# A modulation unit is computed one unit after its load, queued on VectorE behind the last weight unit's low half

## The chip, the core and the metric

The kernel runs on one core of a Trainium2 chip. The metric is the device time of one execution in microseconds (us); a time is the median of several executions. The engines of the core work side by side, each on its own instruction queue in order: PE (TensorE, matrix products), DVE (VectorE), ACT (ScalarE), POOL (GpSimd) and SP (SyncE, which here issues the loads). An instruction waits in its queue until what it needs is there, and everything behind it on the same engine waits with it.

## The reference

Two transformer blocks on 256 tokens of width 2048, all in float32. Each block begins with a modulation: a vector `c` is multiplied with a wide matrix, and the products scale, shift and gate the activations. These products are matrix-vector products; all others have 256 rows.

```python
c_act = silu(c)
mod = c_act @ w_ada + b_ada                      # 2048 x 12288: sh_a, sc_a, gt_a, sh_f, sc_f, gt_f
h = rms_norm(x, g_attn) * (1 + sc_a) + sh_a
x = x + gt_a * parallel_mixers(h, w_in, ..., w_o)  # sparse and dense attention, gated, merged
h = rms_norm(x, g_ffn) * (1 + sc_f) + sh_f
x = x + gt_f * conv_ffn(h, w_up, w_conv, w_down)   # width 5632, 3-tap convolution over tokens
...
shift, scale, gate = split(silu(c_2) @ w_mod + b_mod, 3)   # 2048 x 6144
h = rms_norm(x) * (1 + scale) + shift
x = x + gate * pool_mixer(h, pool_w_in, pool_w_grp, pool_scale, pool_w_out)
out = rms_norm(x) * final_norm_g
```

## The kernel before

**Weight units.** Every weight matrix streams through the core once, in tiles of 128 x 1024 float32 (512 KB: two blocks of 128 rows by 512 columns). One such tile is a weight unit. `load_split` takes a `raw` buffer, loads the tile on SP (L275), lets ScalarE cast it to a high half (L158) and VectorE subtract the high half from the tile, which gives the low half (`tt` in `split`, recorded as L80). Both halves lie in an `hl` buffer. TensorE then does 12 matmuls (L380): two halves of the tokens by two row blocks by three products, high by high, high by low, low by high. There are 564 weight units. The ring of `raw` buffers has 6 (`NRAW`), that of `hl` buffers 5 (`NHL`); a load waits on SP until its `raw` buffer is free, which for a weight unit is when its low half is computed.

**Modulation units.** The matrix-vector products run on VectorE. A modulation unit is one 512 KB tile of `w_ada` or `w_mod`: a `raw` buffer from the same ring, a load on SP (L174), and one fused multiply with row sum on VectorE (L176, `vec_unit`), whose end frees the buffer. There are 288. `job_vec` puts them into the deque `jobs`; after the last unit of a vector it adds the two halves of the sums and calls `fin`, which makes a scale (`A1`, `A2`, `A3`), a shift or a gate row from them. Inside `gemm_gen`, behind each weight unit, `credit` grows by `rate` (0.4 to 1.05, by stage) and `pump(1)` takes one modulation unit for each full credit. `pump_to` and `pump(1000)` take many at once where a vector must be complete.

**What sets the order.** Outside an opening that is written by hand, the scheduler of the Tile framework places each instruction on its engine by its own model of when it can run, not by the line at which the program asks for it. `tc.issue_after(x)` keeps an instruction behind `x` in the queue of the engine, without a wait of its own. Before, a modulation product has one such edge, behind `gate[0]`, a copy in the norm at the start of a stage.

**Stages.** In the order of time: opening and input projection `w_in` (to about 640 us with the attentions; modulation units of `w_ada` at rates 1.05 and 0.5 to 1), `w_o` and the norm of the FFN (to about 740 us), `w_up` and `w_down` interleaved, with the convolution on `cv` tiles (to about 1430 us, modulation units at 0.45 and 0.4), the pool mixer with its input projection into `pu` (split into `puh` and `pul`), the group product `z` and its transpose `zT` (to about 1625 us, rate 0.5), and `pool_w_out`. `hN` are the normalised activations of a stage, high and low halves; `u` is the result of `w_up` ahead of the convolution; `gTlo` the low half of the gated product.

Of the kernel before, what the change touches and what calls it, by code (L numbers as in the profile page):

```python
# [14 lines left out]
OP = mybir.AluOpType  # L15
# [14 lines left out]
def block_pair_kernel(ctx: ExitStack, tc: tile.TileContext, T: dict, out: bass.AP):  # L30
    nc = tc.nc
    V, SC, PE, GP = nc.vector, nc.scalar, nc.tensor, nc.gpsimd
# [9 lines left out]
    NH, RH = 4, 0.9  # L42
    NF = 1
    NS4, NRAW, NHL = 28, 6, 5
    n_s4 = [0]
    WU = (1, 30, 2, 3)

# [31 lines left out]
    def tt(o, a, b, op):  # L79
        return V.tensor_tensor(o, a, b, op=op)  # L80
# [42 lines left out]
    cact = {}  # L123
# [32 lines left out]

    def split(hi, lo, src):
        SC.copy(hi, src)  # L158
        tt(lo, src, hi, OP.subtract)


    jobs = deque()
    gate = [None]

    def pump(n):
        for _ in range(n):
            if not jobs:
                return
            jobs.popleft()()

    def vec_unit(W, ct, h, cv, acc):

        raw = raw_tile()
        nc.sync.dma_start(raw, T[W][ct, h])  # L174
        with tc.issue_after(gate[0]) if gate[0] is not None else nullcontext():
            V.scalar_tensor_tensor(raw, raw, 1.0, cact[cv][h], op0=OP.mult, op1=OP.mult, accum_out=acc)  # L176

    def job_vec(W, cv, cts, fin):

        n = len(cts)  # L180
        st = {}

        def unit(i, h):
            if i == 0 and h == 0:
                n_s4[0] += 1
                st["vs"] = sp.tile([128, 2, 128], F32, name=f"vs_{n_s4[0]}", tag="vs", bufs=2)[:, :, :n]
            vs = st["vs"]
            vec_unit(W, cts[i], h, cv, vs[:, h, i:i + 1])
            if i == n - 1 and h == 1:
                tt(vs[:, 0], vs[:, 0], vs[:, 1], OP.add)  # L190
                fin(vs[:, 0])
        for i in range(n):
            for h in range(2):
                jobs.append(lambda i=i, h=h: unit(i, h))
# [77 lines left out]
    def load_split(blk, n, big=False):  # L272

        raw = raw_tile()
        nc.sync.dma_start(raw[:, :KT * n], blk)  # L275
        rv = raw[:, :KT * n].rearrange("p (k n) -> p k n", k=KT)
        if big:
            hl = [s4([128, KT, 512], F32R, name="hl")[:, :, :n] for _ in range(2)]
        else:
            n_s4[0] += 1  # L280
            t = sp.tile([128, 2, KT, 512], F32R, name=f"hl_{n_s4[0]}", tag="hl", bufs=NHL)
            hl = [t[:, b, :, :n] for b in range(2)]
        split(hl[0], hl[1], rv)
        return hl


# [81 lines left out]
    def gemm_gen(st, W, k0, nk, evac, rate=0.0, tail=0, head=0, kw=None, n=512, pre=(), ps=None,  # L368
                 part=(True, True)):


        ps = ps or [ps_mm(), ps_mm()]
        nu = nk // KT
        u0 = (k0 if kw is None else kw) // KT

        def mms(t, hl, u):
            for i in range(KT):
                k = u * KT + i
                for x, (a, b) in enumerate(((0, 0), (0, 1), (1, 0))):
                    PE.matmul(ps[t][:, :n], lhsT=st(k0 + k, t, a), rhs=hl[b][:, i, :],  # L380
                              start=(part[0] and k == 0 and x == 0), stop=(part[1] and k == nk - 1 and x == 2))
        late = []
        for u in range(nu):
            hl = pre[u] if u < len(pre) else load_split(W[u0 + u], n, big=u >= nu - tail)
            mms(0, hl, u)
            if u >= nu - tail or u < head:
                late.append((hl, u))
            else:
                mms(1, hl, u)
            if u == head - 1:  # L390
                for a in late:
                    mms(1, *a)
                late.clear()
            credit[0] += rate
            while credit[0] >= 1.0:
                pump(1)
                credit[0] -= 1.0
            if u < nu - 1:
                yield
        evac(0, ps[0])  # L400
        for a in late:
            mms(1, *a)
        evac(1, ps[1])
        yield
# [4 lines left out]
    acc = {}  # L409
# [28 lines left out]
    for g in range(NG):  # L438
# [9 lines left out]
        if g == 0:  # L448
# [16 lines left out]
            rest = 2 * math.pi  # L465
# [99 lines left out]
    for q in range(2):  # L565
        a = acc[QI0 + q]
# [14 lines left out]
    for t in range(2):  # L581
# [4 lines left out]
        for b in range(16 // hb):  # L586
            p = ps_at([128, hb, ns], name="dots")
            for i in range(hb):
                h = b * hb + i
# [5 lines left out]
            for i in range(hb):  # L595
                h = b * hb + i
# [8 lines left out]
        for r in range(8):  # L605
            src = score if r == 0 else work
# [35 lines left out]
    for j in range(3):  # L642
        src, c0 = (acc[LAT], j * 256) if j < 2 else (misc, 80)
# [4 lines left out]
        h = t2([128, 2, 256], name="lat32")  # L648
# [10 lines left out]
    for j in range(4):  # L659
        a = s4([128, 2, 384], name="mq")  # L660
        lat_gens.append(gemm_gen(stl, T["w_mq_up"][j], 0, 4, lambda t, p, a=a: SC.copy(a[:, t, :], p[:, :384]),
                                 n=384, rate=R4))
        mq.append(a)
    for j in range(4):
        a = s4([128, 2, 512], name="mkv")
# [28 lines left out]
    for q in range(2):  # L694
        a = acc[Q0 + q]
        rope_a(a, 4, tqa)
        o = s4([128, 4, 256], name="qaT")
        for j in range(2):
            p = ps_tp([128, 2, 256])
            for i in range(2):  # L700
                for t in range(2):
                    h = j * 2 + i
# [22 lines left out]
    for t in range(2):  # L725
        ns = 128 * (t + 1)
        for g in range(2):
            P = s4([128, 4, 256], name="pA")
            hb = 512 // ns
            for b in range(4 // hb):  # L730
                ps = ps_at([128, hb, ns], name="lgA")
                for i in range(hb):
                    h = b * hb + i
# [48 lines left out]
    for t in range(2):  # L782
        j = t2([128, 512], name="junk")
        SC.activation(j[:, :64], misc[:, t, 336:400], AF.Square, accum_out=ssr[:, t:t + 1])
        for jj in range(4):
            for h in range(2):
                j = t2([128, 512], name="junk")
                SC.activation(j[:, :192], mq[jj][:, t, h * 192:(h + 1) * 192], AF.Square,
                              accum_out=ssb[:, 0, t, jj * 2 + h:jj * 2 + h + 1])
# [3 lines left out]
                                       accum_out=ssb[:, 1, t, jj * 2 + h:jj * 2 + h + 1])  # L793
# [334 lines left out]
    for i in range(4):  # L1128
# [14 lines left out]
        for b in range(2):  # L1143
            p = ps_tp([128, 2, 256])
            for q in range(2):
                f = b * 2 + q
                n = 0
# [6 lines left out]
        hi = s4([128, 4, 256], F32R, name="plhi")  # L1154
        lo = s4([128, 4, 256], F32R, name="pllo")
# [162 lines left out]
```

## Time and profile before

| | |
|---|---|
| median of 3 runs | 1737.88 us (1735.26 to 1742.14) |
| profiled execution | 1738.78 us, span 1736.9 us |
| granted TensorE clock, mean | 0.993 |
| busy: PE / DVE / ACT / POOL | 97% / 79% / 52% / 1% |
| moved by DMA | 459.80 MB, mean 265 GB/s |

The span is what the profiler recorded; the execution is 1.9 us longer. Busy shares are means over all stages. "Idle before" in a row is the time in which the engine did nothing just ahead of that instruction, and the name behind the arrow is what ended last before it could start.

### The profile page before, as it was taken

What the parts mean: (1) busy time and instruction counts of PE and PEld (TensorE: products, weight loads), DVE (VectorE), ACT (ScalarE), POOL (GpSimd) and SP (SyncE); (2) the same over time, 40 slices, a digit from 0 to 9 for tenths busy, and PEclk for the clock granted to TensorE, in tenths of its full rate; (3) what the DMA queues carried; (4) which work ended last, traced back from release to release, by engine and by line L of the source; (5) the groups of instructions that cost most, each with busy time, mean ns of one, the idle gap of its engine ahead of it and who ended that gap; (6) DMA issues with size and microseconds to landing.
All of it is one profiled execution on the core that took longest, in us unless ns stands there. A gap on an engine that the chain in (4) does not pass through costs nothing.

```text
span 1736.9 us, 21934 instructions
## 1 busy us (share of the span) xinstructions
PE 1679.3 (97%) x7736; PEld 1375.3 (79%) x7736; DVE 1368.9 (79%) x2079; ACT 906.2 (52%) x1275; POOL 12.7 (1%) x29
## 2 busy tenths in 40 slices
PE   8899999999999989999989999999999999999997
PEld 6688888778778868788878878887888777888886
DVE  8899899998978778599677776777877877765765
ACT  4644354767854456555445544555345575454443
POOL 0000000000000000000000000000000000000000
PEclk9999999999999999999999999999999999999999
DMA  8999998678878858677877787777877748788762
GB/s 326 353 335 328 330 325 282 215 270 302 288 233 316 290 205 320 219 237 245 298 255 256 253 273 261 259 245 257 273 259 253 256 159 263 253 282 271 227 223 92
DMA packets 128834, 459.80 MB, mean 265 GB/s; under 512 B 14626, under 2 KB 16210, under 8 KB 128724
## 3 DMA queue, kind: packets, MB, share of 16 engines
q1 hardware_dynamic: 127380, 454.18, 76.8%
q0 software_dynamic: 1344, 4.22, 0.7%
q8 instruction: 61, 1.00, 0.2%
q14 instruction: 49, 0.40, 0.1%
HBM read 456.22 MB, written 2.12 MB: 264 GB/s over the span
## 4 chain that ended last, share of the span: by engine, by line
PE 55%; DMA 20%; DVE 16%; issue 6%; ACT 2%; SPq 0%; DVEq 0%; POOL 0%; ACTq 0%
PE mm L380 48%; DMA raw<-in_w_mod 11%; DMA raw<-in_w_ada 7%; DVE hl L80 7%; DVE raw L176 3%; PE keep L380 2%; ACT hl L158 1%; PE mm L1183 1%; DVE cv L1033 1%; DVE cv L1035 1%; DMA raw<-in_w_up 1%; DVE score L601 1%; PE tp L1027 1%; DVE cv L80 0%; DVE pacc L80 0%
## 5 line engine op out<-in xcount | busy, mean ns | idle before, releaser
L158 ACT CAST hl<-raw 128x1024 fp32r<-128x1024 f32 (+2 forms) x564 | 586.2, 1046 | 573.4 <-PE mm L380 421.1
L80 DVE TENSOR_TENSOR hl<-raw,hl 128x1024 fp32r<-128x1024 f32 (+2 forms) x564 | 675.8, 1214 | 115.4 <-ACT hl L158 113.4
L380 PE MATMUL mm<-hl,hN 128*128 128x512 f32 x2880 | 674.1, 393 | 9.9 <-DVE hl L80 3.9
L380 PEld LDWEIGHTS mm<-hl,hN 128*128 128x128 f32 x2880 | 539.5, 189 | 123.8 <-DVE hl L80 5.2
L176 DVE SCALAR_TENSOR_TENSOR raw<-raw,cB 128x1024 f32<-128x1024 f32 x288 | 351.2, 1222 | 206.0 <-DMA raw<-in_w_mod 147.6
L380 PE MATMUL mm<-hl,hT 128*128 128x512 f32 (+1 forms) x1248 | 288.8, 390 | 9.7 <-ACT hT L158 3.6
L380 PEld LDWEIGHTS mm<-hl,hT 128*128 128x128 f32 x1248 | 232.5, 188 | 58.8 <-DVE hl L80 4.6
L380 PE MATMUL mm<-hl,gThi 128*128 128x512 f32 x704 | 218.7, 393 | 4.0 <-DVE hl L80 2.1
L380 PEld LDWEIGHTS mm<-hl,gThi 128*128 128x128 f32 x704 | 132.3, 189 | 33.5 <-DVE hl L80 3.3
L380 PE MATMUL mm<-hl,gTlo 128*128 128x512 f32 x352 | 137.6, 394 | 0.8 <-DVE gTlo L80 0.8
L380 PE MATMUL mm<-hl,pair 128*128 128x512 f32 x384 | 89.5, 391 | 0.0
L380 PE MATMUL mm<-hl,zT 128*128 128x512 f32 x384 | 87.5, 389 | 0.0
L380 PEld LDWEIGHTS mm<-hl,zT 128*128 128x128 f32 x384 | 71.9, 188 | 14.9
L380 PEld LDWEIGHTS mm<-hl,pair 128*128 128x128 f32 x384 | 71.5, 188 | 14.6
L380 PEld LDWEIGHTS mm<-hl,gTlo 128*128 128x128 f32 x352 | 66.4, 189 | 15.1 <-DVE gTlo L80 1.6
L1031 ACT ACTIVATE cv<-tp,wcv 128x256 f32<-128x256 f32 x88 | 45.1, 563 | 58.9 <-DVE cv L1035 45.6
L80 DVE TENSOR_TENSOR pacc<-pacc,mm 128x512 f32<-128x512 f32 (+1 forms) x78 | 52.3, 674 | 6.2 <-PE mm L380 5.7
L380 PE MATMUL mm<-hl,oaT 128*128 128x512 f32 x192 | 48.8, 401 | 0.0
L380 PE MATMUL mm<-hl,obT 128*128 128x512 f32 x192 | 47.9, 399 | 0.0
L380 PE MATMUL keep<-hl,hT 128*128 128x512 f32 x192 | 46.0, 396 | 0.8 <-DVE hl L80 0.8
L380 PEld LDWEIGHTS keep<-hl,hT 128*128 128x128 f32 x192 | 36.3, 191 | 9.4 <-DVE hl L80 2.1
L380 PEld LDWEIGHTS mm<-hl,obT 128*128 128x128 f32 x192 | 35.2, 188 | 7.4 <-DVE obT L80 0.4
(337 smaller groups left out, 1181.5 us busy)
## 6 DMA issues: line engine op xcount, KB each, us to landing
raw<-in_w_ada SPq DMA_DIRECT2D x192, 512.0 KB, 4.8
raw<-in_w_up SPq DMA_DIRECT2D x176, 512.0 KB, 4.6
raw<-in_w_in SPq DMA_DIRECT2D x112, 512.0 KB, 5.2
raw<-in_w_mod SPq DMA_DIRECT2D x96, 512.0 KB, 4.5
raw<-in_w_down SPq DMA_DIRECT2D x88, 512.0 KB, 4.5
raw<-in_pool_w_in SPq DMA_DIRECT2D x64, 512.0 KB, 4.5
raw<-in_w_o SPq DMA_DIRECT2D x32, 512.0 KB, 4.8
raw<-in_pool_w_out SPq DMA_DIRECT2D x32, 512.0 KB, 4.3
```

What stands on the lines that cost most here:

```text
L80: return V.tensor_tensor(o, a, b, op=op)
L158: SC.copy(hi, src)
L176: V.scalar_tensor_tensor(raw, raw, 1.0, cact[cv][h], op0=OP.mult, op1=OP.mult, accum_out=acc)
L380: PE.matmul(ps[t][:, :n], lhsT=st(k0 + k, t, a), rhs=hl[b][:, i, :], start=(part[0] and k == 0 and x == 0), stop=(part[1] and k == nk - 1 ...
L601: V.scalar_tensor_tensor(score, r[:, i, :], w, score, op0=OP.mult, op1=OP.add)
L1027: PE.transpose(p[:, i, t * 128:(t + 1) * 128], u[:, t, f * 128:(f + 1) * 128], ident)
L1031: SC.activation(cv[:, f, :], p[:, i, :], AF.Identity, bias=wcv[:, 3, fi:fi + 1], scale=wcv[:, 2, fi:fi + 1])
L1033: V.scalar_tensor_tensor(cv[:, f, 1:], p[:, i, :255], wcv[:, 1, fi:fi + 1], cv[:, f, 1:], op0=OP.mult, op1=OP.add)
L1035: V.scalar_tensor_tensor(cv[:, f, 2:], p[:, i, :254], wcv[:, 0, fi:fi + 1], cv[:, f, 2:], op0=OP.mult, op1=OP.add)
L1183: PE.matmul(pv[:, q, :], lhsT=hls[k // 2][wa][:, k % 2, f * 128:(f + 1) * 128], rhs=pooled[i][xb][:, k, :], start=(k == 0 and x == 0), sto ...
```

## The change

`vec_unit` still takes its buffer and issues its load when `pump` calls it, but gives back a function `compute`. With `lag` 1 (`LAG`, only in the pump of `gemm_gen`) the deque `loaded` keeps one such function back: the product of a modulation unit is asked for when the next unit is loaded. It also gets a second order edge, behind `last_lo[0]`: the low half of the weight unit that was asked for last. `pump` without a lag, as `pump_to` and `pump(1000)` call it, computes what is still held.

```diff
--- before.py
+++ after.py
@@ -42,6 +42,7 @@
     NH, RH = 4, 0.9
     NF = 1
     NS4, NRAW, NHL = 28, 6, 5
+    LAG = 1
     n_s4 = [0]
     WU = (1, 30, 2, 3)
 
@@ -156,24 +157,39 @@
 
     def split(hi, lo, src):
         SC.copy(hi, src)
-        tt(lo, src, hi, OP.subtract)
+        return tt(lo, src, hi, OP.subtract)
 
 
     jobs = deque()
     gate = [None]
 
-    def pump(n):
-        for _ in range(n):
-            if not jobs:
-                return
-            jobs.popleft()()
+    last_lo = [None]
+
+    loaded = deque()
+
+    def pump(n, lag=0):
+
+        for _ in range(min(n, len(jobs))):
+            compute = jobs.popleft()()
+            if compute is not None:
+                loaded.append(compute)
+            while len(loaded) > max(lag, 1):
+                loaded.popleft()()
+        while len(loaded) > lag:
+            loaded.popleft()()
 
     def vec_unit(W, ct, h, cv, acc):
 
         raw = raw_tile()
         nc.sync.dma_start(raw, T[W][ct, h])
-        with tc.issue_after(gate[0]) if gate[0] is not None else nullcontext():
-            V.scalar_tensor_tensor(raw, raw, 1.0, cact[cv][h], op0=OP.mult, op1=OP.mult, accum_out=acc)
+
+        def compute():
+            with ExitStack() as es:
+                for a in (gate[0], last_lo[0]):
+                    if a is not None:
+                        es.enter_context(tc.issue_after(a))
+                V.scalar_tensor_tensor(raw, raw, 1.0, cact[cv][h], op0=OP.mult, op1=OP.mult, accum_out=acc)
+        return compute
 
     def job_vec(W, cv, cts, fin):
 
@@ -185,10 +201,14 @@
                 n_s4[0] += 1
                 st["vs"] = sp.tile([128, 2, 128], F32, name=f"vs_{n_s4[0]}", tag="vs", bufs=2)[:, :, :n]
             vs = st["vs"]
-            vec_unit(W, cts[i], h, cv, vs[:, h, i:i + 1])
-            if i == n - 1 and h == 1:
-                tt(vs[:, 0], vs[:, 0], vs[:, 1], OP.add)
-                fin(vs[:, 0])
+            compute = vec_unit(W, cts[i], h, cv, vs[:, h, i:i + 1])
+
+            def rest():
+                compute()
+                if i == n - 1 and h == 1:
+                    tt(vs[:, 0], vs[:, 0], vs[:, 1], OP.add)
+                    fin(vs[:, 0])
+            return rest
         for i in range(n):
             for h in range(2):
                 jobs.append(lambda i=i, h=h: unit(i, h))
@@ -280,7 +300,7 @@
             n_s4[0] += 1
             t = sp.tile([128, 2, KT, 512], F32R, name=f"hl_{n_s4[0]}", tag="hl", bufs=NHL)
             hl = [t[:, b, :, :n] for b in range(2)]
-        split(hl[0], hl[1], rv)
+        last_lo[0] = split(hl[0], hl[1], rv).ins
         return hl
 
 
@@ -393,7 +413,7 @@
                 late.clear()
             credit[0] += rate
             while credit[0] >= 1.0:
-                pump(1)
+                pump(1, LAG)
                 credit[0] -= 1.0
             if u < nu - 1:
                 yield
```

The changed kernel has the products at L191 and the low halves at L81. Loads keep their order on SP. On VectorE the products move. First place: the FFN at about 880 us of the profile before. `hl` rows are low halves, `u` rows add the second part of a `w_up` product, and the number behind a name's first underscore is the same tile in both. Before:

```order
L176 SCALAR_TENSOR_TENSOR raw_1395_7603,vs_1349_7309<-raw_1395_7603,cB_3_84 128x1024
L80 TENSOR_TENSOR hl_1384_7524<-raw_1383_7522,hl_1384_7524 128x1024
L80 TENSOR_TENSOR hl_1387_7544<-raw_1386_7542,hl_1387_7544 128x1024
L176 SCALAR_TENSOR_TENSOR raw_1402_7657,vs_1349_7309<-raw_1402_7657,cB_4_85 128x1024
L80 TENSOR_TENSOR hl_1394_7588<-raw_1393_7586,hl_1394_7588 128x1024
L80 TENSOR_TENSOR hl_1397_7608<-raw_1396_7606,hl_1397_7608 128x1024
L80 TENSOR_TENSOR hl_1399_7625<-raw_1398_7623,hl_1399_7625 128x1024
L80 TENSOR_TENSOR hl_1401_7642<-raw_1400_7640,hl_1401_7642 128x1024
L80 TENSOR_TENSOR u_1181_6226<-u_1181_6226,mm_1376_7483 128x512
L80 TENSOR_TENSOR u_1181_6226<-u_1181_6226,mm_1377_7484 128x512
```

After:

```order
L81 TENSOR_TENSOR hl_1394_7587<-raw_1393_7585,hl_1394_7587 128x1024
L191 SCALAR_TENSOR_TENSOR raw_1385_7538,vs_1346_7298<-raw_1385_7538,cB_4_85 128x1024
L81 TENSOR_TENSOR hl_1397_7607<-raw_1396_7605,hl_1397_7607 128x1024
L81 TENSOR_TENSOR hl_1399_7624<-raw_1398_7622,hl_1399_7624 128x1024
L81 TENSOR_TENSOR hl_1401_7641<-raw_1400_7639,hl_1401_7641 128x1024
L81 TENSOR_TENSOR u_1181_6222<-u_1181_6222,mm_1376_7482 128x512
L81 TENSOR_TENSOR u_1181_6222<-u_1181_6222,mm_1377_7483 128x512
L191 SCALAR_TENSOR_TENSOR raw_1395_7602,vs_1346_7298<-raw_1395_7602,cB_3_84 128x1024
L81 TENSOR_TENSOR hl_1412_7695<-raw_1411_7693,hl_1412_7695 128x1024
L1053 SCALAR_TENSOR_TENSOR cv_1388_7560<-tp_1389_7561,wcv_73,cv_1388_7560 128x255
L1053 SCALAR_TENSOR_TENSOR cv_1388_7560<-tp_1390_7572,wcv_73,cv_1388_7560 128x255
```

The product of `raw_1402` stood ahead of four low halves and the two `u` additions; after the change that of `raw_1395` stands behind them, and `raw_1402` comes five low halves later still.

Second place: the FFN at about 1188 us, in the convolution of one column block (the L1033/L1035 or L1053/L1055 rows). Before:

```order
L1035 SCALAR_TENSOR_TENSOR cv_1714_9735<-tp_1716_9747,wcv_73,cv_1714_9735 128x254
L176 SCALAR_TENSOR_TENSOR raw_1749_9957,vs_1724_9795<-raw_1749_9957,cB_1416_7730 128x1024
L1033 SCALAR_TENSOR_TENSOR cv_1714_9735<-tp_1715_9736,wcv_73,cv_1714_9735 128x255
L1033 SCALAR_TENSOR_TENSOR cv_1714_9735<-tp_1716_9747,wcv_73,cv_1714_9735 128x255
L1035 SCALAR_TENSOR_TENSOR cv_1714_9735<-tp_1715_9736,wcv_73,cv_1714_9735 128x254
L1035 SCALAR_TENSOR_TENSOR cv_1714_9735<-tp_1716_9747,wcv_73,cv_1714_9735 128x254
L80 TENSOR_TENSOR hl_1734_9855<-raw_1733_9853,hl_1734_9855 128x1024
L80 TENSOR_TENSOR hl_1737_9875<-raw_1736_9873,hl_1737_9875 128x1024
L80 TENSOR_TENSOR hl_1739_9892<-raw_1738_9890,hl_1739_9892 128x1024
L176 SCALAR_TENSOR_TENSOR raw_1754_9994,vs_1724_9795<-raw_1754_9994,cB_1415_7728 128x1024
L80 TENSOR_TENSOR hl_1748_9942<-raw_1747_9940,hl_1748_9942 128x1024
L80 TENSOR_TENSOR hl_1751_9962<-raw_1750_9960,hl_1751_9962 128x1024
```

After:

```order
L1055 SCALAR_TENSOR_TENSOR cv_1714_9731<-tp_1716_9743,wcv_73,cv_1714_9731 128x254
L81 TENSOR_TENSOR hl_1734_9854<-raw_1733_9852,hl_1734_9854 128x1024
L1053 SCALAR_TENSOR_TENSOR cv_1714_9731<-tp_1715_9732,wcv_73,cv_1714_9731 128x255
L1053 SCALAR_TENSOR_TENSOR cv_1714_9731<-tp_1716_9743,wcv_73,cv_1714_9731 128x255
L1055 SCALAR_TENSOR_TENSOR cv_1714_9731<-tp_1715_9732,wcv_73,cv_1714_9731 128x254
L1055 SCALAR_TENSOR_TENSOR cv_1714_9731<-tp_1716_9743,wcv_73,cv_1714_9731 128x254
L191 SCALAR_TENSOR_TENSOR raw_1730_9832,vs_1724_9791<-raw_1730_9832,cB_1416_7729 128x1024
L81 TENSOR_TENSOR hl_1737_9874<-raw_1736_9872,hl_1737_9874 128x1024
L81 TENSOR_TENSOR hl_1739_9891<-raw_1738_9889,hl_1739_9891 128x1024
L81 TENSOR_TENSOR hl_1748_9941<-raw_1747_9939,hl_1748_9941 128x1024
L191 SCALAR_TENSOR_TENSOR raw_1735_9869,vs_1724_9791<-raw_1735_9869,cB_1415_7727 128x1024
L81 TENSOR_TENSOR hl_1751_9961<-raw_1750_9959,hl_1751_9961 128x1024
```

The product of `raw_1749` stood in the middle of the convolution, ahead of `hl_1734`, `hl_1737` and `hl_1739`; there now stands that of `raw_1730`, which was loaded earlier, behind `hl_1734`; `raw_1749` comes behind `hl_1753`.

Third place: the end of the group product of the pool mixer, about 1614 to 1630 us, where `pump(1000)` takes the last four units. `hl_2294` is the first weight unit of `pool_w_out`; in both kernels it stands behind the rows shown. Before:

```order
L80 TENSOR_TENSOR hl_2258_13100<-raw_2257_13098,hl_2258_13100 128x1024
L176 SCALAR_TENSOR_TENSOR raw_2282_13306,vs_2174_12560<-raw_2282_13306,cB_1415_7728 128x1024
L80 TENSOR_TENSOR hl_2265_13166<-raw_2264_13164,hl_2265_13166 128x1024
L1185 SCALAR_TENSOR_TENSOR z32_2250_13032<-mm_2251_13033,colB_69,pgT_2164_12510 128x256
L176 SCALAR_TENSOR_TENSOR raw_2283_13309,vs_2174_12560<-raw_2283_13309,cB_1416_7730 128x1024
L176 SCALAR_TENSOR_TENSOR raw_2284_13312,vs_2174_12560<-raw_2284_13312,cB_1415_7728 128x1024
L1185 SCALAR_TENSOR_TENSOR z32_2250_13032<-mm_2251_13033,colB_69,pgT_2164_12510 128x256
L1185 SCALAR_TENSOR_TENSOR z32_2250_13032<-mm_2253_13063,colB_69,pgT_2164_12510 128x256
L176 SCALAR_TENSOR_TENSOR raw_2285_13315,vs_2174_12560<-raw_2285_13315,cB_1416_7730 128x1024
L80 TENSOR_TENSOR zT_2252_13060<-z32_2250_13032,zT_2252_13060 128x512
L80 TENSOR_TENSOR vs_2174_12560<-vs_2174_12560 128x8
L1185 SCALAR_TENSOR_TENSOR z32_2250_13032<-mm_2253_13063,colB_69,pgT_2164_12510 128x256
```

After:

```order
L1205 SCALAR_TENSOR_TENSOR z32_2268_13173<-mm_2269_13174,colB_69,pgT_2217_12842 128x256
L1205 SCALAR_TENSOR_TENSOR z32_2268_13173<-mm_2271_13204,colB_69,pgT_2217_12842 128x256
L191 SCALAR_TENSOR_TENSOR raw_2242_13003,vs_2171_12549<-raw_2242_13003,cB_1416_7729 128x1024
L191 SCALAR_TENSOR_TENSOR raw_2282_13305,vs_2171_12549<-raw_2282_13305,cB_1415_7727 128x1024
L1205 SCALAR_TENSOR_TENSOR z32_2268_13173<-mm_2269_13174,colB_69,pgT_2217_12842 128x256
L1205 SCALAR_TENSOR_TENSOR z32_2268_13173<-mm_2271_13204,colB_69,pgT_2217_12842 128x256
L191 SCALAR_TENSOR_TENSOR raw_2283_13308,vs_2171_12549<-raw_2283_13308,cB_1416_7729 128x1024
L81 TENSOR_TENSOR zT_2270_13201<-z32_2268_13173,zT_2270_13201 128x512
L81 TENSOR_TENSOR zT_2272_13231<-z32_2268_13173,zT_2272_13231 128x512
L1205 SCALAR_TENSOR_TENSOR z32_2277_13244<-mm_2278_13245,colB_69,pgT_2243_13008 128x256
L1205 SCALAR_TENSOR_TENSOR z32_2277_13244<-mm_2280_13275,colB_69,pgT_2243_13008 128x256
L191 SCALAR_TENSOR_TENSOR raw_2284_13311,vs_2171_12549<-raw_2284_13311,cB_1415_7727 128x1024
```

Before, four products (`raw_2282` to `raw_2285`) stand between the first `z` rows, with `hl_2267`, `hl_2274` and `hl_2276` behind them; after, five products (`raw_2242` too) stand behind `hl_2276`, between later `z` rows and ahead of `hl_2294`.

## Rows read from the trace of the kernel before

**Rows 1.** Page: the span; busy time, share and instructions of each engine.
```profile
span 1736.9 us, 21934 instructions
...
PE 1679.3 (97%) x7736; PEld 1375.3 (79%) x7736; DVE 1368.9 (79%) x2079; ACT 906.2 (52%) x1275; POOL 12.7 (1%) x29
```

**Rows 2.** Waits of all engines: who waits for whom, us in total, times, longest.
```profile
ACT hl L158 <- PE mm L380: 421.1, 275, 3.8
DVE raw L176 <- DMA raw<-in_w_mod: 147.6, 75, 6.2
...
ACT hl L158 <- DMA raw<-in_w_in: 77.4, 53, 3.4
DVE raw L176 <- DMA raw<-in_w_ada: 57.9, 41, 6.4
```

**Rows 3.** Timeline of PE, ten places: start, length, what, [idle before <-releaser].
```profile
334.72 1.66 PE L380 MATMUL mm<-hl,hT 128*128 128x512 f32 x6 [0.91 <-DVE hl L80]
...
735.96 6.41 PE L380 MATMUL mm<-hl,hN 128*128 128x512 f32 x27 [1.52 <-DVE hN L80]
...
886.36 0.69 PE L1027 MATMUL tp<-cst,u 128*128 128x128 f32 x2 [3.11 <-DVE u L80]
...
1192.10 2.25 PE L380 MATMUL mm<-hl,hN 128*128 128x512 f32 x6 [2.36 <-DVE hl L80]
...
1353.60 2.58 PE L380 MATMUL mm<-hl,hN 128*128 128x512 f32 x10 [1.28 <-DVE hl L80]
...
1373.44 0.50 PE L380 MATMUL mm<-hl,gThi 128*128 128x512 f32 x1 [2.08 <-DVE hl L80]
...
1446.24 4.15 PE L380 MATMUL mm<-hl,hN 128*128 128x512 f32 x17 [1.19 <-DVE hN L80]
...
1460.36 0.50 PE L1150 MATMUL tp<-bwr,puh 128*128 128x256 f32 x2 [1.13 <-ACT puh L158]
...
1475.08 0.50 PE L1150 MATMUL tp<-bwr,puh 128*128 128x256 f32 x2 [1.54 <-ACT puh L158]
...
1622.58 0.50 PE L1183 MATMUL mm<-plhi,hl 128*128 128x256 f32 x2 [1.18 <-DVE z L1185]
```

**Rows 4.** Timeline of PE in a full stretch: first and last of 20 starts.
```profile
999.64 0.39 PE L380 MATMUL mm<-hl,gThi 128*128 128x512 f32 x1
...
1003.94 0.39 PE L380 MATMUL mm<-hl,gTlo 128*128 128x512 f32 x1
```

**Rows 5.** Timeline of VectorE ahead of the PE gap at 886 us.
```profile
879.92 1.23 DVE L176 SCALAR_TENSOR_TENSOR raw<-raw,cB 128x1024 f32<-128x1024 f32 x1 [6.44 <-DMA raw<-in_w_ada]
...
885.62 1.28 DVE L80 TENSOR_TENSOR u<-u,mm 128x512 f32<-128x512 f32 x2
```

**Rows 6.** Groups by line: VectorE and ScalarE work on 512 KB tiles.
```profile
L80 DVE TENSOR_TENSOR hl<-raw,hl 128x1024 fp32r<-128x1024 f32 (+2 forms) x564 | 675.8, 1214 | 115.4 <-ACT hl L158 113.4 <-DMA raw<-in_w_pb 0.8
...
L158 ACT CAST hl<-raw 128x1024 fp32r<-128x1024 f32 (+2 forms) x564 | 586.2, 1046 | 573.4 <-PE mm L380 421.1 <-DMA raw<-in_w_in 77.4 <-DMA raw<-in_w_up 21.1
...
L176 DVE SCALAR_TENSOR_TENSOR raw<-raw,cB 128x1024 f32<-128x1024 f32 x288 | 351.2, 1222 | 206.0 <-DMA raw<-in_w_mod 147.6 <-DMA raw<-in_w_ada 57.9
```

**Rows 7.** Windows: stretch, us, PE, PEld, DVE, ACT, POOL busy (x), PEclk, DMA, GB/s.
```profile
95.00:175.00 80.00, 80.00 (x360) 66.96 (x359) 76.40 (x105) 35.00 (x37) 0.31 (x1) 1.00 0.93 334
175.00:265.00 90.00, 90.00 (x408) 75.59 (x407) 84.67 (x131) 42.12 (x49) 0.31 (x1) 1.00 0.92 325
...
640.00:940.00 300.00, 290.61 (x1305) 237.93 (x1304) 229.75 (x325) 164.42 (x216) 2.13 (x4) 0.99 0.75 255
940.00:1375.00 435.00, 426.51 (x1904) 347.29 (x1903) 323.70 (x428) 206.01 (x242) 1.07 (x2) 0.99 0.78 259
...
1430.00:1625.00 195.00, 189.22 (x902) 155.97 (x901) 135.29 (x163) 95.06 (x112) 1.07 (x2) 1.00 0.78 262
```

**Rows 8.** DMA issues: kind, count, size each, median us to landing.
```profile
raw<-in_w_in SPq DMA_DIRECT2D x112, 512.0 KB, 5.2
```

**Rows 9.** Waits of the SP queue, which issues the loads.
```profile
SPq L275 <- DVE raw L176: 276.0, 130, 7.3
```

## The prediction

> **What bounds the kernel now.** I read the page first: PE is busy 97% of the span, VectorE 79%, ScalarE 52% [rows 1]. Busy time of PE is modelled, so I checked a stretch: between the first and the last of 20 matmul starts lie 4.30 us, 0.226 us for each [rows 4]. A weight unit of 12 matmuls takes 2.72 us, and in whole stretches, as from 95 to 265 us, PE stands at 80.00 of 80.00 and 90.00 of 90.00 us [rows 7]. What can be won is idle time of PE: 1736.9 − 1679.3 = 57.6 us in all [rows 1].
>
> Next the chain of releasers behind that idle time, in the table of waits. VectorE waits 147.6 + 57.9 = 205.5 us, in 116 waits, for the load of a modulation unit [rows 2]. That is far more than the 57.6 us that PE loses, so most of it is hidden. The same table says by what: ScalarE's casts wait 421.1 us for PE to free an `hl` buffer [rows 2], so the weights usually lie ready ahead of PE, up to five units or 13.6 us. A wait on VectorE of 2 to 6 us ends there unseen, unless something stands behind it in the queue that PE needs at once.
>
> So I went through PE's timeline for gaps, and for each looked at VectorE's timeline just before. The clearest: VectorE waits 6.44 us for a `w_ada` tile and computes it at 879.92 us; four low halves and the two additions of `u` (from 885.62) stand behind it; PE stands still for 3.11 us until `u` is there, at 886.36 [rows 3, 5]. Gaps of this kind with a modulation wait in the queue ahead: 3.11 at 886, 2.36 at 1192, 1.28 at 1353, 2.08 at 1373, 1.13 at 1460, 1.54 at 1475, and in part 1.52 at 735, 1.19 at 1446, 0.91 at 334 and 1.18 at 1622 [rows 3].
>
> **The change part by part.** It adds and removes no instruction of weight: 288 products of 1.222 us on VectorE [rows 6] stay 288, loads stay in their order on SP. The edges of order cost nothing by themselves, since they are satisfied in the queue.
>
> *The products move back.* The three places of the order show how far: not one weight unit but some five low halves in the FFN, because before the scheduler had put the product early, about where it was loaded. Five weight units are 5 × 2.72 = 13.6 us of PE's time. The longest wait there was 6.4 us [rows 2], so the tile has landed long before its turn and VectorE no longer waits for it. Both ends: the saving can't be below nothing at a gap and not above the gap. I take the whole gap where the product or its wait is the only late thing in front: 3.11 + 2.36 + 1.28 + 2.08 + 1.13 + 1.54 = 11.5 us [rows 3]. At 735 and 1446 us what PE waits for is `hN`, which hangs on the norm as well; one product goes on standing just ahead of it. I take half: (1.52 + 1.19) / 2 = 1.4 us. At 334 us the low halves now stand ahead of work of the top-k selection, and 0.9 us goes.
>
> *The end of the group product.* Before, four products stand between the `z` rows, and PE waits 1.18 us at 1622 [rows 3]; that goes. But five products now stand ahead of `hl_2294`, the first low half of the next matrix, where none stood. They are 5 × 1.222 = 6.1 us of work on VectorE. The cost lies between nothing, if this unit is far enough ahead, and 6.1 us. The `z` chain is a run of short steps from PE to VectorE and back, in which VectorE has pauses that take a part; I take 2.6 us lost, a little under the middle, for two products in the pauses and one behind the lead of one unit (6.1 − 2 × 1.222 − 1.2 = 2.5).
>
> *The flush in the opening.* Where `pump_to` completes `A1` at about 68 us, one held product more stands in the burst ahead of a low half for which PE waits: 0 to 1.2 us, I take 1.2 [rows 6].
>
> *The vector held longest.* When the jobs of a vector run out under the lag, the last product waits for the next flush; `A2` becomes ready 19 low halves later. It is needed only for the norm of the FFN (the gap at 735 us), where the new order still has it ahead of `hN` by four low halves. I cost it at nothing beyond the half gain there; without that cover it would cost some 1.2 us.
>
> *The ring.* A modulation tile now holds its `raw` buffer until its later product. So fewer of the six are left for weights. By counting in the new order which low half frees the buffer of which load, a weight load in the FFN was issued about five low halves ahead and is now nearly four; in units 41 to 160 of the input projection it was about four and is now mostly three. Three units give 3 × 2.72 = 8.16 us for the round: landing 5.2 us [rows 8], cast 1.05 us, subtraction 1.21 us [rows 6], together 7.46 us. VectorE's other work of a unit fits into the flight. In the FFN four units give 10.9 us. I cost it at nothing; in the opening only 0.7 us of margin hides it.
>
> Sum: −11.5 − 1.4 − 0.9 − 1.2 + 2.6 + 1.2 = −11.2 us. Against the profiled execution, 1738.8 − 11.2 = 1727.6 us; that execution lies 0.9 us above the median of the runs shown, so I predict 1727 us.
>
> **The rivals.**
>
> *The stalls are made again elsewhere (no change).* VectorE must still do 1.222 us for each product, and the moved ones stand ahead of other things: in the new order three stand in a row at the end of the FFN, ahead of the residual. For it: VectorE is busy 324 of 435 us in that window and the gaps of PE there are only 8.5 us in all [rows 7], so a gap taken from one place can be eaten by the next short chain. Against: most waits were hidden before by the same lead. If only the two clearest chains profit, 3.11 at 886 and 1.13 at 1460, and the two losses come (3.8), the sum is −0.4: 1737 us, with −5 to +5 around it.
>
> *The ring runs short in the opening (slower).* For it: SP already waits 276.0 us, 130 times, for a modulation product before it can load a weight [rows 9], in the input projection ScalarE waits 53 times for the weight tile itself [rows 2], and VectorE is busy 84.67 of 90 us [rows 7], 2.56 us of each unit's 2.72, of which 1.21 is the low half. If its other 1.35 us fall into the round and not beside the flight, the round is 7.46 + 1.35 = 8.81 us, which over three units is 2.94 us, 0.22 us too long; over the 120 units 41 to 160 that is 26 us. Some 5 us of lead and the 11 us gained elsewhere go off: +10, 1748 us as a median. It decides from a round of 8.16 us on. Against: PE was never short of a weight there, and with fewer loads under way each should land sooner. [...]
>
> *More than forecast.* All idle time of PE in the windows from 640 to 940, 940 to 1375 and 1430 to 1625 us goes, 9.4 + 8.5 + 5.8 = 23.7 us [rows 7], with 0.9 us at 334: 1713 us as a median. Against: norms and transposes in these windows wait for PE itself.
>
> *The change doesn't do what it says.* The product lands some five low halves later, not one; if the scheduler's place on the chip left it waiting still, nothing would change. The tile would have to take over 13 us to land; I count this with the first rival.
>
> **How the numbers follow.** Chances: forecast 0.43, stalls made again 0.33, ring short 0.15, more 0.09. Half a per cent, 8.7 us, is about what a measurement of this kernel can tell from no change: faster means below 1729.2, slower above 1746.6 us. The forecast's own range is 1721 us (neither loss comes, 3.8, and the halves go whole, 1.4) to 1734 us (the loss at the group product is 6.1 instead of 2.6, and two of the six gaps, 3.6, stay); some four fifths of it, by chance, lie below 1729.2. Faster: 0.34 + 0.09 = 0.43; slower: 0.14 of the ring's 0.15; the rest, 0.43, is the same. The range for 8 in 10 reaches from 1712, which takes in most of the third rival, to 1747, which leaves out about half of the ring's case.
>
> **What would show it.** Right: VectorE's waits for modulation loads fall from 205.5 us to below 40; PE has no gap above 0.5 us at the six places counted whole; the low halves ahead of the group product's end are late by 2 to 3 us at about 1620 us; VectorE's busy time is unchanged. Wrong by the first rival: those waits are gone, and PE's busy share stays at 97% with new gaps near the old ones. Wrong by the ring: ScalarE's casts wait longer for `w_in` loads than 77.4 us [rows 2], the windows from 95 to 265 us no longer show PE full, and the input projection ends later. What would upset the forecast most is a returning gap of a few tenths in each unit of the opening, for it is multiplied by over a hundred.

## The result and the profile after

The changed kernel takes 1722.9 us (median of 4 runs, 1722.22 to 1723.91), the one before 1739.83 us in the same comparison. The ratio is 0.9908, with an interval from 0.9884 to 0.9933: faster by 0.9%. The forecast was 1727 us, in a range from 1712 to 1747. Of all executions below one, of e2, took 4581.76 us: it is left out of e2's ratio, and it counts in e2's median as the highest of five (the median of the other four is 1710.4 us).

The page of the changed kernel, and its waits (engine, line waited for: us in total, times, longest):

```profile
span 1720.1 us, 21829 instructions
...
PE 1676.5 (97%) x7736; PEld 1374.8 (80%) x7736; DVE 1374.6 (80%) x2079; ACT 909.4 (53%) x1275; POOL 13.8 (1%) x29
```

```profile
ACT hl L159 <- PE mm L400: 422.7, 284, 4.0
DVE hl L81 <- ACT hl L159: 287.0, 281, 5.6
...
ACT hl L159 <- DMA raw<-in_w_in: 107.2, 66, 5.0
```

The two rows of VectorE's waits for modulation loads, 205.5 us together [rows 2], are no longer in the list. The group of the products says the same, with no idle time left ahead of them:

```profile
L191 DVE SCALAR_TENSOR_TENSOR raw<-raw,cB 128x1024 f32<-128x1024 f32 x288 | 349.4, 1217 | 0.0
```

Busy time is within 6 us of what it was on every engine. VectorE now waits for casts instead (287.0 us), which is harmless where the casts wait for PE. On SP the loads kept their order but for some swaps: 17 of the 883 issues stand in another place, 13 of them at the start of the pool stage. One row went the wrong way: ScalarE waits 107.2 us for `w_in` tiles, before 77.4 us [rows 2]. The windows of the changed kernel (stretch, us, busy of PE, PEld, DVE, ACT, POOL, PEclk, DMA, GB/s):

```profile
95.00:175.00 80.00, 80.00 (x359) 66.94 (x359) 75.98 (x103) 35.19 (x37) 0.31 (x1) 1.00 0.93 331
175.00:265.00 90.00, 90.00 (x406) 75.63 (x405) 84.29 (x127) 40.61 (x46) 0.31 (x1) 1.00 0.93 326
...
640.00:940.00 300.00, 294.81 (x1321) 241.39 (x1320) 233.88 (x328) 167.64 (x220) 2.13 (x4) 0.99 0.77 257
940.00:1375.00 435.00, 435.00 (x1962) 356.97 (x1961) 338.42 (x445) 214.29 (x250) 1.07 (x2) 1.00 0.81 267
```

From 940 to 1375 us PE is busy 435.00 of 435.00 us, before 426.51 [rows 7].

Where the time went is best read by matching matmuls. Both kernels have 7736 PE records, in nearly the same order, so the start of the n-th record in one trace minus its start in the other gives what was won or lost up to there. In us, after minus before, each from the profiled execution:

| up to record | start before | after | reading |
|---|---|---|---|
| 400 | 107.58 | +4.01 | lost in the opening, up to 95 us |
| 1400 | 325.26 | +4.00 | nothing in the full stretch |
| 3300 | 734.04 | +7.71 | lost in the attention stages |
| 4200 | 938.34 | +1.05 | won at 736, 886 and 901 us |
| 6000 | 1346.49 | −7.44 | won in the FFN |
| 7300 | 1633.63 | −21.50 | won in the FFN's end and the pool mixer |
| 7700 | 1718.80 | −16.89 | lost behind the group product |

So, between these two executions, 29.2 us were won and 12.3 us lost (7.7 and 4.6); how much of that another execution repeats is a question for the experiments. The loss at the end stands in the timelines, VectorE's first and then PE's:

```profile
1616.94 1.22 DVE L191 SCALAR_TENSOR_TENSOR raw<-raw,cB 128x1024 f32<-128x1024 f32 x1
...
1618.09 1.22 DVE L191 SCALAR_TENSOR_TENSOR raw<-raw,cB 128x1024 f32<-128x1024 f32 x1
...
1620.34 1.22 DVE L81 TENSOR_TENSOR hl<-raw,hl 128x1024 fp32r<-128x1024 f32 x1
```

```profile
1616.69 0.50 PE L1203 MATMUL mm<-plhi,hl 128*128 128x256 f32 x2 [0.69 <-DVE z L1205]
...
1621.62 1.78 PE L400 MATMUL mm<-hl,zT 128*128 128x512 f32 x6 [1.79 <-DVE hl L81]
```

The last products end at 1619.2 us, the low half of the output matrix that PE waits for comes at 1620.34, and that wait is 1.79 us.

### The profile page after: what moved, and what is told of

It is laid out like the page before. It is cut to its first block, busy times and chain, and to the rows that moved or that the text cites. A ratio compares the mean times of both kernels' runs of the same rounds, so it can differ in the third digit from the quotient of the medians.

```text
span 1720.1 us, 21829 instructions
## 1 busy us (share of the span) xinstructions
PE 1676.5 (97%) x7736; PEld 1374.8 (80%) x7736; DVE 1374.6 (80%) x2079; ACT 909.4 (53%) x1275; POOL 13.8 (1%) x29
## 4 chain that ended last, share of the span: by engine, by line
PE 70%; issue 11%; DVE 10%; DMA 5%; ACT 4%; POOL 0%; ACTq 0%; DVEq 0%; POOLq 0%; SPq 0%
PE mm L400 64%; DVE hl L81 3%; DMA raw<-in_w_in 3%; DVE raw L191 2%; ACT hl L159 2%; PE mm L1203 1%; PE tp L1047 1%; DVE pacc L81 1%; PE tp L1170 0%; PE cb L104 0%; PE tp L944 0%; DVE score L621 0%; DMA raw<-in_w_mkv_up 0%; DMA raw<-in_w_pb 0%; DMA raw<-in_w_pa 0%
## 5 line engine op out<-in xcount | busy, mean ns | idle before, releaser
L81 DVE TENSOR_TENSOR hl<-raw,hl 128x1024 fp32r<-128x1024 f32 (+2 forms) x564 | 681.8, 1214 | 288.3 <-ACT hl L159 287.0
L191 DVE SCALAR_TENSOR_TENSOR raw<-raw,cB 128x1024 f32<-128x1024 f32 x288 | 349.4, 1217 | 0.0
L81 DVE TENSOR_TENSOR pacc<-pacc,mm 128x512 f32<-128x512 f32 (+1 forms) x78 | 51.8, 671 | 1.8 <-PE mm L400 1.6
L400 PEld LDWEIGHTS mm<-hl,oaT 128*128 128x128 f32 x192 | 34.9, 188 | 7.6 <-DVE hl L81 0.6
```

## The experiments

All kernels are the changed one with an edit, but e7, which is the kernel before with one. The distance of a product is counted in the order: how many low halves stand ahead of it on VectorE, less the weight loads ahead of its own load on SP. Zero means right behind the low half of the weight unit after which it was loaded. The means over the 55 products of the larger part of the FFN:

| kernel | distance | median, us | ratio to before (interval) |
|---|---|---|---|
| before | −3.1 | 1734.55 to 1739.83, by comparison | 1 |
| changed | +2.2 | 1722.9 | 0.9908 (0.9884 to 0.9933) |
| e1, lag and edge from the FFN on | +2.2 | 1716.49 | 0.9877 (0.9856 to 0.9898) |
| e2, edge without lag | 0.0 | 1711.32 | 0.9849 (0.9827 to 0.987) |
| e3, lag without edge | −3.1 | 1736.96 | 0.9998 (0.9981 to 1.0015) |
| e4, changed, 7 raw buffers | +2.2 | 1714.94 | 0.9874 (0.9854 to 0.9894) |
| e5, lag of two | +4.3 | 1774.22 | 1.023 (1.0206 to 1.0253) |
| e6, changed, pool rate 0.6 | +2.1 | 1717.3 | 0.9903 (0.9885 to 0.9921) |
| e7, before, 7 raw buffers | −4.1 | 1729.17 | 0.9973 (0.996 to 0.9986) |
| e8, e2 with 7 buffers and rate 0.6 | 0.0 | 1706.47 | 0.9842 (0.9824 to 0.986) |
| e9, lag and edge up to the FFN | −3.1 | 1742.65 | 1.0027 (1.001 to 1.0043) |
| e10, e2 with 7 buffers | 0.0 | 1706.46 | 0.9825 (0.9799 to 0.9852) |

The kernel before was run again beside each group of experiments (e1 to e4, e5 to e8, e9 and e10). Its single executions lie between 1729 and 1746 us, so across groups the ratio, which is taken over the runs and not from the two medians, is the safer comparison. By their intervals the ratios of the changed kernel, e1, e4 and e6 can't be told apart.

The theory after the result (theory A in the expectations): a product that stands on VectorE ahead of the place at which its load was issued waits for the load and holds up the low halves behind it; moved behind that place it waits no more. What it costs (theory R) is the `raw` buffer, held until the product is done. The rivals: the two traces differ by chance of the order; or it is the lag of one unit that does it.

**e1, from the FFN on.**

```diff
-    LAG = 1
+    LAG = [0]
+    edge = [False]
...
-                for a in (gate[0], last_lo[0]):
+                for a in (gate[0], last_lo[0] if edge[0] else None):
...
-                pump(1, LAG)
+                pump(1, LAG[0])
...
+    LAG[0], edge[0] = 1, True
     rB = norm_rows(ss1, pre1, "rn1")
```

> The lag and the edge behind the last low half are used only from the norm of the FFN on; up to there the order on every engine is that of the kernel before. Theory A (the gain comes from the FFN and pool stages, where a product no longer stands ahead of its load; the changed kernel loses 4.0 us in the opening up to 95 us and 3.7 us in the attention stage, by the matmul starts matched one by one): the 7.7 us come back, about 1715 us, and VectorE waits for modulation loads only before 640 us. Theory B (the differences of the stages are chance of the order and do not add up): 1720 to 1727 us, like the changed kernel.

1716.49 us: theory A's number within 1.5 us. By ratio the gain over the changed kernel (0.9877 against 0.9908) is about 5 us, and the intervals overlap. All waits of VectorE for modulation loads lie before 640 us, as theory A said:

```profile
DVE raw L192 <- DMA raw<-in_w_ada: 19.7, 22, 2.1
```

In the matched starts the opening costs 0.62 us in place of 4.01; between there and the FFN another 3.3 us were lost in this profile although the order there is that of before, so the early stages scatter by some 3 us from one execution to the next, and the 3.7 us of the attention stages are not shown as one cause's.

**e9, up to the FFN**, the complement: `LAG = [1]`, `edge = [True]`, and at the norm `pump(0)` and `LAG[0], edge[0] = 0, False`.

> The complement of e1_late: lag and edge up to the norm of the FFN, the order of the kernel before from there on. Theory A with losses of 4.0 us in the opening and 3.7 us in the attention stage: 1741 to 1746 us, ratio about 1.004, waits of VectorE for modulation loads only behind 640 us, about 150 us. Rival (the early losses were chance of one profile): 1733 to 1739 us, ratio 0.998 to 1.002.

Slower than before by 6.3 us, ratio 1.0027, clear of 1 though not by much. VectorE waits again, and all of it behind 640 us:

```profile
DVE raw L192 <- DMA raw<-in_w_mod: 145.8, 72, 6.5
...
DVE raw L192 <- DMA raw<-in_w_ada: 34.5, 19, 4.4
```

So the change is a loss ahead of the FFN and a gain from the FFN on. The two parts multiply to the whole within the scatter: 0.9877 × 1.0027 = 0.9904, against 0.9908.

e9 is also a second execution of the order of before: from 735 us on, PE, VectorE, ScalarE and SP have the same instructions in the same order as in the kernel before. Yet its gaps lie elsewhere. At 886 us of before there is none in e9, at 1192 there is 1.28 us in place of 2.36, and these are larger than before (1.27 at 901, 0.54 at 1215):

```profile
906.64 0.42 PE L1050 MATMUL tp<-cst,u 128*128 128x128 f32 x2 [2.44 <-DVE u L82]
...
1221.59 2.55 PE L401 MATMUL mm<-hl,gThi 128*128 128x512 f32 x6 [2.06 <-ACT gThi L160]
```

Which of VectorE's waits reaches PE is thus a matter of the single execution; what repeats is the sum. From record 3300 to record 7300 (734 to 1634 us of before) the profiles take 899.6 us before, 893.5 in e9, and 889.0 and 886.7 in e3 and e7 below, which also have their products ahead of the loads' place. All eight kernels that have them at or behind it take 869.7 to 873.3 us, whatever the distance. Measured against e9, the changed kernel wins 23.1 us there in place of 29.2.

**e2, edge without lag, and e3, lag without edge.** e2 sets `LAG = 0`; e3 leaves `last_lo[0]` out:

```diff
-                for a in (gate[0], last_lo[0]):
+                for a in (gate[0],):
```

> Each product is computed without lag, right behind the low half of the weight unit it was loaded behind; counted in the order, the product stands 0 low halves from its load's place, where before it stood 3 low halves ahead in the FFN and after the change 2.2 to 2.5 behind. Theory A (what counts is that the product no longer stands ahead of its load; the cast and the low half, 2.3 us, cover most of the rest of the flight): waits of VectorE for modulation loads below 40 us, 1712 to 1720 us, since buffers are held less long. Theory of the text (one unit of lag is what hides the load): most of the waits come back, over 100 us, and 1728 to 1738 us.

> The lag without the edge behind the last low half. In the order the scheduler puts the products back to 3 low halves ahead of their loads' place in the FFN. Theory A: no gain, 1735 to 1742 us, waits of VectorE for modulation loads again about 200 us. Rival (asking one unit later is enough): below 1730 us.

These two tell most. Alone, the edge does more than the change; alone, the lag does nothing, because without the edge the scheduler puts the product back to where it stood, 3.1 low halves early. The waits, of e2 and then of e3:

```profile
DVE raw L191 <- DMA raw<-in_w_ada: 2.8, 1, 2.8
```

```profile
DVE raw L191 <- DMA raw<-in_w_mod: 145.9, 75, 4.2
...
DVE raw L191 <- DMA raw<-in_w_ada: 51.8, 41, 4.0
```

At distance 0 one wait of 2.8 us is left of 116. The durations fit: the tile is loaded right behind a weight tile, and while that weight tile is cast and subtracted (1.05 + 1.21 us [rows 6]) the modulation tile can land too. Further back buys nothing: the ratios of e2 and of the changed kernel are apart by their intervals. From record 3300 to 7300 the two are alike (873.3 and 870.4 us); e2 gains ahead of it (+0.51 us at 734 us, the changed kernel +7.71) and loses less at the end (0.96 us, not 4.6). e2 ran at 1711.32 us, a little better than expected.

**e4, e7 and e5: the ring.** `NS4, NRAW, NHL = 28, 6, 5` becomes `27, 7, 5` in e4 and, in the kernel before, in e7; e5 sets `LAG = 2`.

> The changed kernel with seven raw buffers in place of six and 27 general buffers in place of 28. Theory R (its loss of 4.0 us before 95 us is a ring run short, since modulation tiles hold buffers longer): the loss goes, about 1718 us, and ScalarE waits for w_in loads fall from 107.2 us to below 80. Rival (the loss is one product more in the burst ahead of the flush, work and not room): the time stays at 1723 us or within 2 us of it.

> The kernel before with seven raw buffers and 27 general ones, the control for the ring. Theory R (before was not short of buffers; only the held tiles of the change make it so): no change, ratio 0.997 to 1.003. Rival (a seventh buffer helps any of these kernels by the 8 us that it gave the changed one): about 1729 us, ratio 0.995.

> The changed kernel with a lag of two units: products stand 4.3 to 5.2 low halves behind their loads' place from the output projection of the attention block (w_o) on, and 1.9 to 2.8 before it. Theory R (a held buffer is what the change costs; the loss before 95 us and in the attention stage grows with each buffer held): 1728 to 1745 us, with ScalarE's waits for weight loads well above the 107.2 us for w_in of the changed kernel. Rival (buffers are ample; only the burst at the flush costs): 1720 to 1726 us, one product more at the flush.

e4 is faster by 8 us than the changed kernel by the medians (6 us by the ratios, whose intervals overlap), and the waits for `w_in` fall below those of before:

```profile
ACT hl L159 <- DMA raw<-in_w_in: 64.0, 41, 3.3
```

Its opening costs 2.01 us in the matched starts in place of 4.01, so about half of that loss looks like room, by one profile of each (the burst ahead of the flush, which the seventh buffer leaves, was not tried by itself). But e7 speaks against theory R as it was put: the kernel before gains 5.4 us from the seventh buffer as well. Its ratio, 0.9973, is at the edge of the range given for theory R, but the interval leaves out 1, and the rival's 1729 us is what came. Its waits:

```profile
DVE raw L176 <- DMA raw<-in_w_mod: 109.8, 73, 4.4
...
ACT hl L158 <- DMA raw<-in_w_in: 40.5, 26, 3.1
```

The ring was a little short already. That the change makes it shorter shows in ScalarE's waits; that the seventh buffer gives the changed kernel more than it gives before is not shown (0.34% against 0.27%). In e7 the products stand further ahead of their loads' place than before (−4.1) and yet wait less (157.7 us), so the distance alone does not set how long the waits are. e5 is the strong case. With two units held it is 2.3% slower than before, by far more than expected, and the waits for weights are these:

```profile
ACT hl L159 <- DMA raw<-in_w_in: 151.1, 84, 4.7
ACT hl L159 <- DMA raw<-in_w_up: 97.0, 59, 4.8
```

The windows of the opening, full in both kernels, are full no more, while the FFN still is:

```profile
95.00:175.00 80.00, 77.23 (x340) 62.83 (x339) 69.40 (x109) 33.02 (x37) 0.31 (x1) 1.00 0.86 293
175.00:265.00 90.00, 81.92 (x337) 61.39 (x336) 75.98 (x106) 36.34 (x40) 0.31 (x1) 1.00 0.87 293
940.00:1375.00 435.00, 435.00 (x1961) 356.69 (x1960) 339.88 (x444) 216.30 (x250) 1.07 (x2) 1.00 0.80 266
```

And PE's timeline in the opening has the returning gap, one every few units:

```profile
187.75 5.94 PE L400 MATMUL mm<-hl,hT 128*128 128x512 f32 x24 [0.48 <-DVE hl L81]
...
194.37 3.01 PE L400 MATMUL mm<-hl,hT 128*128 128x512 f32 x12 [0.69 <-DVE hl L81]
...
197.98 3.26 PE L400 MATMUL mm<-hl,hT 128*128 128x512 f32 x12 [0.59 <-DVE hl L81]
...
201.99 11.64 PE L400 MATMUL mm<-hl,hT 128*128 128x512 f32 x48 [0.76 <-DVE hl L81]
```

Matched with before, e5 has lost 8.60 us at 108 us, 27.6 at 325 and 50.2 at 734, then wins back 27 in the FFN and the pool mixer like the others, and loses 8.0 at the end of the group product. The returning gap that the prediction feared most has come, of 0.48 to 0.76 us though not in each unit, and ScalarE waits 151.1 us for `w_in` tiles, 107.2 with one unit held. That more buffers would close it was not tried. So e5 is the prediction's slower rival, one held unit later than it was feared.

**e6, e8 and e10: the end, and the best version.** e6 sets the three rates of the pool stage from 0.5 to 0.6, so that four of the five products are done before the late `z` rows. e8 is e2 with both edits, e10 is e2 with the ring alone.

> The changed kernel with the rate of the pool stage at 0.6 in place of 0.5, so that four of the five products that stood between the late z rows are done before. Theory (the five products cost 4.6 us there): 1718 to 1720 us, no wait of PE for the first low half of the output matrix. Rival (PE waits there for z anyway): 1722 to 1724 us.

> Edge without lag, seven raw buffers and the pool rate of 0.6 together. If the parts add up: some 1.7 us of the opening and 1 us at the end come off 1711 us, 1707 to 1710 us. Rival (with no lag the buffers are not held, so the seventh does nothing, and the end costs little already): 1710 to 1713 us, the same as the edge alone.

> The edge without lag and seven raw buffers, pool rate 0.5 as before: which part of e8 gave the 4.8 us over e2. If the buffer gave them (the kernel before gained 5 us from it too): 1706 to 1708 us. If the early jobs gave them (0.96 us of loss at the end in e2 and the products' own place): 1710 to 1712 us.

e6 took 1717.3 us, and PE runs into the output matrix without a wait:

```profile
1614.83 1.78 PE L400 MATMUL mm<-hl,zT 128*128 128x512 f32 x7
```

In the matched starts it goes from −22.04 to −22.07 us there, where the changed kernel went from −21.50 to −16.89. The 4.6 us come from those five products. (By ratio, 0.9903 against 0.9908, the runs do not tell e6 from the changed kernel; the matched starts do.) On top of the edge and the ring the same edit gives nothing that the medians show (e8 and e10 agree within 0.1 us): without the lag four products are left over, not five, and e2's end costs only 0.96 us. e10, 1706.46 us, beats both kernels: its ratio to before is 0.9825 (0.9799 to 0.9852), and it takes 16 us less than the changed kernel. Its opening costs nothing (−0.45 us in the matched starts).

## Why the prediction was right

**What bounds it.** Right: PE is the bound, and only what stands between VectorE's waits and PE counted. 205.5 us of waits went away, and with them 29.2 us of PE's time in the profiles shown (23.1 against e9).

**The products move back.** The mechanism was right, and the gaps at 886, 1192, 1353, 1373, 1460 and 1475 us are gone. The size was not right. The sum took 11.5 us, the length of the six gaps; matched starts give 4.6 + 4.3 + 1.4 + 3.8 + 1.4 + 1.8 = 17.3 us. What was missing is PE's clock. Windows of the kernel before, ahead of a long gap, with the gap, just behind it and later (PEclk is the third number from the end):

```profile
1183.00:1189.00 6.00, 6.00 (x28) 4.98 (x27) 3.10 (x6) 1.96 (x3) 0.00 (x0) 1.00 0.72 237
1189.00:1193.00 4.00, 1.64 (x8) 1.03 (x7) 4.00 (x8) 2.00 (x3) 0.00 (x0) 0.99 0.40 131
1193.00:1196.00 3.00, 3.00 (x9) 2.35 (x8) 1.80 (x3) 1.89 (x2) 0.00 (x0) 0.50 0.89 257
1197.00:1202.00 5.00, 5.00 (x25) 4.11 (x23) 3.15 (x3) 2.23 (x4) 0.00 (x0) 1.00 0.90 316
```

The gap ends at 1192.10. From about 1193 us the granted clock is 0.50, and from 1197 us on 1.00 again. Behind the gaps of 3.11 and 2.08 us it is 0.54 (886.4 to 889.4 us) and 0.50 (1374 to 1377 us); in the 3 us behind each of those of 1.28, 1.13 and 1.54 us it is 1.00. After the gap of 2.36 us six matmuls took 2.25 us; after that of 1.28 us ten took 2.58 us [rows 3]. So the three gaps above 2 us (3.11, 2.36, 2.08) cost 12.7 us in place of 7.6, and the shorter three 4.6 in place of 4.0.

Two cautions. The gaps are those of one execution: e9, with the same order from 735 us on, lacks the one at 886, and so does e3. So the place by place account is in part that execution's luck; what the change takes away is the sum. And the granted clock did not always fall behind such a gap (last section).

The rest of the difference are places that the text had not counted: 901 (1.5 us), 1005 to 1008 (2.0), 1173 (0.6), 1215 (1.5) and 1420 to 1424 us (2.1; two gaps, of 0.98 and 1.20 us, stand there in both kernels, but the granted clock from 1375 to 1430 us was 0.92 before and is 1.00), together 7.7 us. The text had looked for a modulation wait just ahead of a gap. At 901 us it lies 11 us earlier, and at 1005 and 1215 us PE waits for the gated product of ScalarE and VectorE, one step further along the chain. The halves at 736 and 1446 us came to 1.9 against 1.4, the `z` rows to 2.1 against 1.2. At 334 us the 0.9 us did not come: PE waits there for low halves in both.

**The losses.** Both places were named, both too small. The end of the group product cost 4.6 in place of 2.6 us; e6 shows that it is the five products. PE's two waits there, 0.69 and 1.79 us, are 2.5 us, close to the term. The rest again goes with the clock: e1 has the same two waits, keeps its clock, and loses 3.1 us (e4: 3.0). The changed kernel behind the wait, then the same wait in e1 with its window:

```profile
1623.00:1626.00 3.00, 3.00 (x10) 2.22 (x8) 3.00 (x3) 1.50 (x3) 0.52 (x1) 0.51 0.78 228
```

```profile
1618.04 1.67 PE L401 MATMUL mm<-hl,zT 128*128 128x512 f32 x6 [1.79 <-DVE hl L82]
```

```profile
1618.00:1624.00 6.00, 5.96 (x26) 4.81 (x27) 6.00 (x8) 2.79 (x4) 0.52 (x1) 1.00 0.84 267
```

The flush in the opening stood at 1.2 in the sum; the opening as a whole lost 4.0 us (5.3 and 6.2 in the profiles of e9 and e6, which have the lag there too), perhaps half of it room in the ring (e4), which the text had costed at nothing with a margin of 0.7 us. From 325 to 734 us 3.7 us more went, which no term of the sum had. e9 shows that the early part loses, 6.3 us, and the opening alone can be all of it: e1 loses 3.3 us between 107 and 734 us with the order of before, so a loss of the change in the attention is not shown.

In all, 29.2 won and 12.3 lost against 15.0 and 3.8 (23.1 won, against e9). The text's gains were too small by a factor of 1.5 to 2 and its losses by one of 3. These errors partly cancel, and that the total came within 6 us of the measured one is to that extent luck.

**The rivals.** The stalls were not made again elsewhere (e2, e6). The ring did run short, at the edge as the text said, and its rival's full form is e5. What stood against it, that loads would land sooner, came to 0.2 us: from 95 to 265 us the `w_in` loads landed in 5.1 us, before in 5.3 (medians). "More than forecast" was right about the stages (24.6 us expected there, 29.2 won, or 23.1 against e9) and wrong in that it had no losses. That the products land five low halves later, and not one unit, was right, and e2 shows that it is further than needed.

## What to carry to other kernels

On an engine with an in-order queue, look where an instruction that waits for a load stands in relation to the place at which the load was issued; a scheduler may put it ahead. Move it behind the work that was loaded just before it, and no further: the order edge alone took 205.5 us of waits to 2.8, and each further unit of lag held a buffer and cost time where the ring had little room: with one unit the ratio was 0.9908 in place of 0.9849, with two 1.023. A gap seen in one profile need not be in the next, so count them as a sum and repeat the profile. Count a gap of the matrix engine with what its clock can give away behind it: here three gaps of 2.08 to 3.11 us, with the clock at 0.50 to 0.54 behind them, cost 12.7 us in place of 7.6.

## What the runs showed of the hardware

In the kernel before, the granted clock was 0.50 to 0.54 just behind three gaps of PE of 2.1 to 3.1 us, and they cost 1.5 to 1.9 us more than their own length; behind three gaps of 1.1 to 1.5 us it was 1.00, and they cost about their length, within 0.3 us.

The length of the gap alone does not decide it. Behind the wait of 1.79 us at the end of the group product the clock was 0.51 in the changed kernel and stayed at 1.00 in e1, and the place cost 4.6 us in the one and 3.1 in the other. Behind the same two gaps of 0.98 and 1.20 us at the end of the FFN it was 0.50 before and 1.00 after:

```profile
1419.00:1425.00 6.00, 5.97 (x15) 4.57 (x16) 5.66 (x17) 5.91 (x17) 0.00 (x0) 0.50 0.34 122
```

```profile
1403.00:1409.00 6.00, 4.09 (x18) 2.60 (x18) 5.57 (x23) 5.44 (x15) 0.00 (x0) 1.00 0.42 131
```

In the changed kernel, without gaps from 940 to 1375 us, the clock stands at 1.00 there; in the kernel before it is 0.50 just behind the gap of 2.36 us.
